# Weights split ahead of time into DRAM, and convolution taps summed in PSUM by TensorE and VectorE

## The chip, the cores and the metric

The program runs on one core of a Trainium2 chip. Its time is the device time of one execution in microseconds (us), and a version is judged by the median of several such executions. Engines are named as in the profile: PE (TensorE), DVE (VectorE), ACT (ScalarE), POOL (GpSimd), SP (SyncE, which here only issues transfers); PEld are PE's weight loads.

## The reference, cut to what matters

Two transformer blocks follow one another on 512 tokens of 1024 features, all in float32. The stage that the change is about is the pooling and convolution mixer of the second block; beside it, the keys and values of the memory for the second cross attention come from `m @ wkv`.

```python
def pool_conv_mixer(h, w_in, pool_w, pool_scale, dw_w, dw_b, ln_g, ln_b, w_out):
    z = h @ w_in                                        # 1024 -> 512 + 512 + 512
    u, glu_a, glu_b = jnp.split(z, [POOL_W, POOL_W + CONV_W_2], axis=-1)
    ug = u.reshape(b, t, N_POOL_GROUPS, POOL_GROUP)     # 4 groups, windows 2, 4, 8, 16
    pooled = jnp.stack([window_mean_minus_self(ug[:, :, i], w) ...], axis=2)
    ya = jnp.einsum("btgc,gcd->btgd", pooled, pool_w).reshape(b, t, POOL_W) * pool_scale
    gl = glu_a * jax.nn.sigmoid(glu_b)
    cv = causal_dwconv(gl, dw_w) + dw_b                 # 31 taps for each of 512 channels
    yb = jax.nn.silu(layernorm(cv, ln_g, ln_b))
    return jnp.concatenate([ya, yb], axis=-1) @ w_out
...
    k, v = jnp.split(m @ wkv, 2, axis=-1)               # m: 256 rows of normed memory
```

The stages in order are mix1, ffn1 (first block), pool, xa0, ffn2a, mla, xa1, ffn2b with the output (second block).

## The kernel before

Activations are feature-major: a tile holds 128 features by 512 tokens. A float32 product is made of three products in a reduced float32 (fp32r): each operand is split into a high part `hi` and a low part `lo`, and `mm3` (L239 to L242) sums hi·hi, lo·hi and hi·lo in PSUM. So each weight block is loaded by SP (`ws`, L228), then split: ACT writes `wh` (L211), DVE writes `wl` (L212); `ws`, `wh` and `wl` have three buffers each. A scheduler places the instructions of each engine; the splits are given a priority ahead of the products that need them (`AHEAD`, 150 steps in the pool stage).

**ffn1** (`ffn`, L1193) runs over 22 blocks of 128 hidden features. Each takes a gate and an up block (24 products each), a three-tap convolution, a gelu and a product; then eight output blocks of 66 products follow (`PostNorm`), three weight loads each. `PostNorm.apply` then takes the norm of the result: PE sums squares (L300), a power gives the factor per token, PE spreads it over the partitions (`bcast_cols`, L321), DVE and POOL scale (L477), DVE adds x (L479), and ACT and DVE split the next stage's operand into `nh` (L217) and `nl` (L218), tile by tile.

**The pool stage** (`pool_mix`, L1240) needs twelve column blocks of `w_in`, in the order of `ORDER`: `p` is a pooling group, `g` a pair of gate and value blocks of the convolution, `w` a product with `pool_w`. For a group g POOL makes the window sums (L1295), DVE subtracts (L1300), and `ph`/`pl` are split. For a convolution channel block, the gated tile `gl` (L1260) is summed over 31 taps: DVE takes 87 taps of the four blocks in SBUF (L1279), POOL takes 29 of its own (L1277), ACT the first and the last. When `cv` of all four is there, PE sums them over the channels (L1345, four matmuls against a matrix of ones), ACT and DVE make the layer norm with another sum of squares and another spreading, and the result is split again (`ypart`) for the output product `residual`. PSUM has eight banks: six for blocks (`mm`), two for sums (`aux`).

**Memory K/V of the second layer** (`mem_kv` with `plain=True`) are plain float32 products of 256 columns: eight blocks of K (L633), four of V (L645). They are PE's filling work: `PNF`, `PFILL` and `LNF` say after which step of `apply`, of the pool stage and of the layer norm a piece is emitted. Their weights go through `ws`; results are stored in DRAM (L619).

SP issues all of these loads and stores in one row; one that must wait (for a free buffer, or for data to be stored) holds back all behind it.

## Time and profile before

| | us |
|---|---|
| median of three runs | 2208.73 (2205.94 to 2208.89) |
| span of the profiled execution | 2204.3 |
| PE busy | 2107.7 (96%) |
| DVE busy | 1251.6 (57%) |
| ACT busy | 931.9 (42%) |
| POOL busy | 419.4 (19%) |

The profiled execution is one of its own; its span lies 1.6 us under the fastest and 4.4 us under the median of the timed runs. PE is busy nearly everywhere, so what counts are the stretches where it is not. The table of stretches gives, for each, the time in which PE had work; the timeline gives each gap with what ended it. The pool stage runs from 760.8 us (the last product of ffn1) to 991.8 us (the last product of its output).

### The profile page before, as it was taken

The page shows a single profiled execution, that of the slowest core. Times are in us where ns is not written, and L with a number is a line of the kernel's source. Part 1 is how long each engine was busy: PE and PEld are TensorE (multiplying, and loading weights), DVE is VectorE, ACT ScalarE, POOL GpSimd, SP SyncE. Part 2 cuts the span into 40 slices and gives each one's busy share as a digit, 9 for nine tenths or more (in the row PEclk, how much of TensorE's full clock was granted, in tenths as well). Part 3 has the DMA queues.
Part 4 walks back from the last instruction along what each step waited for, and adds up shares of the span by engine and source line. Part 5 has one row for each costly group of instructions (what it writes and reads, how often), then busy time and mean ns, then how long its engine had stood idle before and what let it go on. Part 6 is the DMA issues. An engine that isn't in the chain of part 4 may idle for free.

```text
span 2204.3 us, 27463 instructions
## 1 busy us (share of the span) xinstructions
PE 2107.7 (96%) x10615; PEld 1779.8 (81%) x10615; DVE 1251.6 (57%) x1796; ACT 931.9 (42%) x1527; POOL 419.4 (19%) x437
## 2 busy tenths in 40 slices
PE   8999999999999987799999999999999999999998
PEld 6988888788888865688888888888888888888887
DVE  6556864655542189955665554337885565555432
ACT  5675444433333253253443333225774343333322
POOL 2114422211100156420111110012322011111010
PEclk9999999999999998899999999999999999999999
DMA  5443235233333232372133333332124213333231
GB/s 162 144 154 104 77 109 178 87 96 96 96 98 112 83 115 62 101 229 86 53 91 96 97 100 98 114 106 56 27 82 157 86 49 92 99 96 96 89 104 66
DMA packets 369983, 222.86 MB, mean 101 GB/s; under 512 B 22407, under 2 KB 351036, under 8 KB 369852
## 3 DMA queue, kind: packets, MB, share of 16 engines
q1 hardware_dynamic: 366304, 219.65, 33.0%
q8 instruction: 83, 1.36, 0.3%
q10 hardware_dynamic: 3228, 1.42, 0.2%
q14 instruction: 48, 0.39, 0.1%
q0 software_dynamic: 320, 0.04, 0.0%
HBM read 201.41 MB, written 19.66 MB: 100 GB/s over the span
## 4 chain that ended last, share of the span: by engine, by line
PE 48%; DVE 4%; ACT 3%; issue 2%; POOL 1%; DMA 0%; SPq 0%; POOLq 0%; ACTq 0%; DVEq 0%
PE mm L242 13%; PE mm L240 13%; PE mm L241 13%; PE st L240 1%; PE st L241 1%; PE st L242 1%; PE nd L240 1%; PE nd L241 1%; PE nd L242 1%; ACT pr L1648 1%; DVE wl L212 1%; DVE c L1647 1%; PE aux L321 0%; DVE ptl L212 0%; DVE qt L212 0%
## 5 line engine op out<-in xcount | busy, mean ns | idle before, releaser
L211 ACT ACTIVATE wh<-ws 128x1024 fp32r<-128x1024 f32 (+2 forms) x336 | 344.8, 1028 | 747.9 <-PE mm L242 548.5
L212 DVE TENSOR_TENSOR wl<-ws,wh 128x1024 fp32r<-128x1024 f32 (+2 forms) x336 | 405.9, 1208 | 314.1 <-ACT wh L211 314.1
L240 PE MATMUL mm<-a,wh 128*128 128x512 f32 x1324 | 520.7, 393 | 0.8 <-ACT a L217 0.8
L242 PE MATMUL mm<-a,wh 128*128 128x512 f32 x1324 | 518.4, 392 | 1.1 <-DVE a L218 1.1
L241 PE MATMUL mm<-a,wl 128*128 128x512 f32 x1324 | 518.0, 391 | 0.3 <-DVE wl L212 0.2
L242 PEld LDWEIGHTS mm<-a,wh 128*128 128x128 f32 x1324 | 249.3, 188 | 54.1 <-DVE a L218 3.0
L240 PEld LDWEIGHTS mm<-a,wh 128*128 128x128 f32 x1324 | 249.7, 189 | 52.2 <-ACT a L217 1.7
L241 PEld LDWEIGHTS mm<-a,wl 128*128 128x128 f32 x1324 | 249.8, 189 | 51.6 <-DVE wl L212 1.0
L286 POOL TENSOR_TENSOR sq<-sq 128x512 f32<-128x512 f32 x62 | 98.8, 1594 | 632.0 <-ACT sq L281 530.9
L240 PE MATMUL mm<-hh,wh 128*128 128x512 f32 (+1 forms) x550 | 209.8, 381 | 0.0
L241 PE MATMUL mm<-hh,wl 128*128 128x512 f32 (+1 forms) x550 | 209.5, 381 | 0.0
L242 PE MATMUL mm<-hl,wh 128*128 128x512 f32 (+1 forms) x550 | 209.4, 381 | 0.0
L1223 POOL TENSOR_TENSOR t<-t,rb 128x512 f32<-128x512 f32 x66 | 85.3, 1293 | 626.5 <-ACT t L1222 626.5
L1210 DVE TENSOR_TENSOR t<-mm,rb 128x512 f32<-128x512 f32 x66 | 45.6, 691 | 152.3 <-PE mm L242 152.2
L1226 DVE TENSOR_TENSOR t<-mm,t 128x512 f32<-128x512 f32 x66 | 45.6, 692 | 143.4 <-POOL t L1223 143.4
L241 PEld LDWEIGHTS mm<-hh,wl 128*128 128x128 f32 x550 | 103.4, 188 | 19.7
L242 PEld LDWEIGHTS mm<-hl,wh 128*128 128x128 f32 x550 | 103.4, 188 | 19.7
L240 PEld LDWEIGHTS mm<-hh,wh 128*128 128x128 f32 x550 | 103.4, 188 | 19.7
L1219 DVE SCALAR_TENSOR_TENSOR t<-t,par 128x511 f32<-128x511 f32 (+1 forms) x132 | 98.7, 748 | 3.2 <-ACT t L1215 0.9
L1222 ACT ACTIVATE t<-t 128x512 f32<-128x512 f32 x66 | 41.7, 632 | 132.1 <-DVE t L1219 132.0
L1279 DVE SCALAR_TENSOR_TENSOR cv<-gl,par,cv 128x512 f32<-128x512 f32 x87 | 90.1, 1077 | 0.4
L240 PE MATMUL mm<-wh,a 128*128 128x256 f32 x282 | 82.2, 292 | 6.2 <-DVE f L838 3.9
(442 smaller groups left out, 3668.8 us busy)
## 6 DMA issues: line engine op xcount, KB each, us to landing
ws<-in_ffn_w_up_dram SPq DMA_DIRECT2D x110, 512.0 KB, 3.7
ws<-in_ffn_w_down_dram SPq DMA_DIRECT2D x48, 512.0 KB, 3.5
ws<-in_xa_wkv_dram SPq DMA_DIRECT2D x32, 512.0 KB, 4.1
ws<-in_w_in_dram SPq DMA_DIRECT2D x24, 512.0 KB, 5.0
ws<-in_ffn_w_gate_dram SPq DMA_DIRECT2D x22, 512.0 KB
ws<-in_ffn_w_down_dram SPq DMA_DIRECT2D x24, 384.0 KB, 3.0
ws<-in_xa_wq_dram SPq DMA_DIRECT2D x16, 512.0 KB, 5.6
ws<-in_xa_wo_dram SPq DMA_DIRECT2D x16, 512.0 KB, 3.5
```

The costliest lines, as they stand in the source:

```text
L211: SC.activation(out=hi, in_=src, func=ACTF.Copy)
L212: eng.tensor_tensor(out=lo, in0=src, in1=hi.bitcast(F32), op=ALU.subtract)
L240: PE.matmul(ps, lhsT=lh, rhs=rh, start=start, stop=False)
L241: PE.matmul(ps, lhsT=ll, rhs=rh, start=False, stop=False)
L242: PE.matmul(ps, lhsT=lh, rhs=rl, start=False, stop=stop)
L286: GP.tensor_tensor(out=self.acc, in0=self.acc, in1=self.new, op=ALU.add)
L1210: V.tensor_tensor(out=g, in0=pg, in1=rb, op=ALU.mult)
L1219: V.scalar_tensor_tensor(out=cv[:, o], in0=g[:, i], scalar=w, in1=cv[:, o], op0=ALU.mult, op1=ALU.add)
L1222: SC.activation(out=ge, in_=cv, func=func)
L1223: GP.tensor_tensor(out=ge, in0=ge, in1=rb, op=ALU.mult)
L1226: V.tensor_tensor(out=h, in0=pu, in1=ge, op=ALU.mult)
L1279: V.scalar_tensor_tensor(out=cv, in0=gl[:, j:j + S], scalar=w, in1=cv, op0=ALU.mult, op1=ALU.add)
```

## The change

- While ffn1 runs, 32 blocks are split ahead of time (`split_ahead`): the twelve of the pool stage's `w_in`, the four double tiles of the normed memory with the layer's gain, eight of K's weights and eight halves of V's. Each is loaded into `rs`, split (ACT into `rh`, DVE in place) and stored in DRAM as high and low part; there is one `rs` and one `rh`. One block is handled with each of the 22 gate/up blocks, the other ten with the output blocks.
- In the pool stage `get_halves` loads the two parts straight into `wh` and `wl` (for K's weights both into `ws` buffers): no split there. `pool_w` and `w_out` are still split there.
- Memory K/V are fp32r products by `mm3`: three of 256 columns for each float32 one before; the work is still PE's filling.
- `apply` calls `pool_open` after each tile: the first three `w_in` blocks (8, 4, 9) take the tile at once, in PSUM banks of their own (`op`). The final factor of the norm follows after the eighth tile.
- The convolution is summed in a PSUM bank (`cv`, two of them; `mm` has four in that stage): for the second to fourth channel block PE adds 5, 5 and 6 taps, each as one float32 product of a diagonal matrix (made by ACT) with the shifted `gl`; DVE adds its 24, 19, 19 and 18 taps with the PSUM bank as input and output; POOL has six taps of each block.
- The channel sums are made one by one, as each `cv` is there (`means`). The tables `ORDER`, `PNF`, `PFILL`, `TAPS` and `LNF` are new.

```diff
+PEC = (0, 5, 5, 6)
+ORDER = 'a1 b2 a2 b3 a3 p0 p2 p1 w0 p3 w2 w1 w3'
...
+    def split_ahead(pool, items):
+        for key, src, gains in items:
+            if callable(src):
+                src = src()
+            nk, n = src.shape[1], src.shape[2]
+            st = pool.tile([P, nk, n], F32, tag="rs", bufs=1, name="rs")
+            hi = pool.tile([P, nk, n], F32R, tag="rh", bufs=1, name="rh")
+            DMA.dma_start(out=st, in_=src)
+            lo = st.bitcast(F32R)
+            if gains is None:
+                split(hi, lo, st)
+            else:
+                for i, g in enumerate(gains):
+                    split(hi[:, i], lo[:, i], st[:, i], g)
+            yield
+            d = [dramp.tile([P, nk, n], F32, name=f"{key[0]}{z}" + "_".join(map(str, key[1:])))
+                 for z in "hl"]
+            DMA.dma_start(out=d[0], in_=hi.bitcast(F32))
+            DMA.dma_start(out=d[1], in_=st)
+            halves[key] = d
+            yield
+    def get_halves(key, kinds=("wh", "wl")):
+        ts = []
+        for d, kind in zip(halves[key], kinds):
+            t = w_tile(kind, d.shape, F32R)
+            DMA.dma_start(out=t.bitcast(F32), in_=d)
+            ts.append(t)
+        return ts
...
+                if each:
+                    each(nm, c)
+            if not each:
+                return nm.finish()
+            self.fill(2 * KD + 3)
+            r = nm.ss.rstd(D)
+            self.fill(2 * KD + 4)
+            nm.finish(r)
+            self.fill(2 * KD + 5)
+            return nm
...
+    def kv_ahead(l):
+        w = A["xa_wkv_2"][l]
+        for k in range(KD // 2):
+            yield (("mem", l, k), lambda k=k: mem_x[k], [pc("mem", KD * l + 2 * k + z) for z in range(2)])
+        for c in range(KD):
+            yield ("kw", l, c), w[:, c * P:(c + 1) * P].rearrange("(k p) c -> p k c", p=P), None
+        for c in range(4):
+            for k in (0, 4):
+                yield (("vw", l, c, k), w[k * P:(k + 4) * P, D + c * 2 * P:D + (c + 1) * 2 * P]
+                       .rearrange("(k p) c -> p k c", p=P), None)
...
+    def mem_kv_ahead(l, tag):
+        parts = []
+        for k in range(KD // 2):
+            hl = [act_tile((P, 2, 2 * P)) for _ in range(2)]
+            for t, d in zip(hl, halves["mem", l, k]):
+                DMA.dma_start(out=t.bitcast(F32), in_=d)
+            parts.extend((hl[0][:, z], hl[1][:, z]) for z in range(2))
+        yield
...
+            wh, wl = get_halves(("kw", l, c), ("ws", "ws"))
+            ps = pm(tag, (P, 2 * P))
+            for k in range(KD):
+                mm3(ps, wh[:, k, :], wl[:, k, :], *parts[k], k == 0, k == KD - 1)
...
+                wh, wl = get_halves(("vw", l, c, k0))
+                for t in range(2):
+                    ts = slice(t * P, (t + 1) * P)
+                    for k in range(4):
+                        ah, al = parts[k0 + k]
+                        mm3(ps[:, t], ah[:, ts], al[:, ts], wh[:, k, :], wl[:, k, :],
+                            k0 + k == 0 and t == 0, k0 + k == KD - 1 and t == 1)
...
             for f in range(KF):
                 pg = lin_f(wg, f * P, parts)
+                drain(pre, 1)
...
                 hs.append((hh, hl))
+                drain(pre, 1)
...
+            def both(i):
+                if i < KD:
+                    drain(pre, 2 if i < KD - 1 else None)
+                (fill or (lambda i: None))(i)
...
+        psum_phase(op=3, mm=3, aux=2)
+        return pn.apply(nxt, None, pp[0], pool_open)
...
+    def pool_ahead():
+        wi = A["pc_w_in_2"][0]
+        for c in (8, 4, 9, 5, 10, 6, 11, 7, 0, 2, 1, 3):
+            yield ("pw", c), wi[:, c * P:(c + 1) * P].rearrange("(k p) c -> p k c", p=P), None
+    def pool_products(blk, k, nm):
+        ps, (wh, wl) = blk
+        mm3(ps, wh[:, k, :], wl[:, k, :], *nm.parts[k], k == 0, k == KD - 1)
+    def pool_open(nm, k):
+        if k == 0:
+            opened.extend((pm("op"), get_halves(("pw", c))) for c in (8, 4, 9))
+        for blk in opened:
+            pool_products(blk, k, nm)
...
+        own = {c: {1 + i * 30 // POOLC[c] for i in range(POOLC[c])} for c in range(4)}
+        dia = {c: [j for j in range(1, 31) if j not in own[c]][:PEC[c]] for c in range(4)}
+        def conv_pe(c):
+            gl = gls[c]
+            cps[c] = pm("cv")
+            for n, j in enumerate(dia[c]):
+                dg = pp.tile([P, P], F32, tag="dgc", bufs=3, name="dgc")
+                SC.activation(out=dg, in_=ident, func=ACTF.Copy, scale=pc("dw_w", 4 * j + c))
+                PE.matmul(cps[c], lhsT=dg, rhs=gl[:, j:j + S], start=n == 0,
+                          stop=n == PEC[c] - 1)
+        def conv(c):
+            gl, ps = gls[c], cps[c]
+            c2 = pp.tile([P, S], F32, tag="c2", bufs=2, name="c2")
+            SC.activation(out=c2, in_=gl[:, 0:S], func=ACTF.Identity, scale=pc("dw_w", c),
+                          bias=pc("dw_b", c))
+            fresh = not PEC[c]
+            for j in range(1, 31):
+                w = pc("dw_w", 4 * j + c)
+                if j in own[c]:
+                    t = pp.tile([P, S], F32, tag="cm", bufs=4, name="cm")
+                    SC.activation(out=t, in_=gl[:, j:j + S], func=ACTF.Copy, scale=w)
+                    GP.tensor_tensor(out=c2, in0=c2, in1=t, op=ALU.add)
+                elif j in dia[c]:
+                    continue
+                elif fresh:
+                    V.tensor_scalar(out=ps, in0=gl[:, j:j + S], scalar1=w, scalar2=None,
+                                    op0=ALU.mult)
+                    fresh = False
+                else:
+                    V.scalar_tensor_tensor(out=ps, in0=gl[:, j:j + S], scalar=w, in1=ps,
+                                           op0=ALU.mult, op1=ALU.add)
+                yield
...
-            V.tensor_tensor(out=cv, in0=cv, in1=c2, op=ALU.add)
+            V.tensor_tensor(out=cv, in0=ps, in1=c2, op=ALU.add)
...
+        def means():
+            while len(sums) < len(cvs):
+                c = len(sums)
+                if c == 0:
+                    means.ps = pm("aux")
+                sums.append(c)
+                PE.matmul(means.ps, lhsT=ones, rhs=cvs[c], start=c == 0, stop=c == 3)
...
-            psum_phase(mm=6, aux=2)
+            psum_phase(mm=4, cv=2, aux=2)
```

How the instructions stand. First SP within ffn1, gate/up blocks. Before, with what each waits for (DMAHW: an earlier transfer landed; DVE, Activation: that engine is done with a tile):

```order
L227 DMA ws<-in_ffn_w_up_dram 128x8x128 [waits DMAHW2_49,DMAHW1_49,DVE_49]
L227 DMA ws<-in_ffn_w_gate_dram 128x8x128 [waits DMAHW3_49,DVE_49]
L227 DMA ws<-in_ffn_w_up_dram 128x8x128 [waits DMAHW6_49,DVE_49]
L227 DMA ws<-in_ffn_w_gate_dram 128x8x128 [waits DMAHW4_49,DMAHW1_49,DVE_49]
L227 DMA ws<-in_ffn_w_up_dram 128x8x128 [waits DMAHW5_49,DMAHW2_49,DVE_49]
L227 DMA ws<-in_ffn_w_gate_dram 128x8x128 [waits DMAHW3_49,DVE_49]
```

The same place now; `rs` and `rh` are the single buffers, `pwh`/`pwl` the parts in DRAM:

```order
L227 DMA ws<-in_ffn_w_up_dram 128x8x128 [waits DMAHW5_49,DVE_49]
L251 DMA rs<-in_pc_w_in_dram 128x8x128 [waits DMAHW6_49,DMAHW4_49]
L227 DMA ws<-in_ffn_w_gate_dram 128x8x128 [waits DMAHW0_49,DVE_49]
L261 DMA pwh_4481<-rh 128x1024 [waits Activation_49]
L262 DMA pwl_4482<-rs 128x1024 [waits DMAHW1_49,DVE_49]
L227 DMA ws<-in_ffn_w_up_dram 128x8x128 [waits DMAHW2_49,DVE_49]
L251 DMA rs<-in_pc_w_in_dram 128x8x128 [waits DMAHW3_49,DMAHW1_49]
L227 DMA ws<-in_ffn_w_gate_dram 128x8x128 [waits DMAHW5_49,DVE_49]
```

Between two weight loads there now stand a load of `rs` that waits for the two stores ahead of it to land, or two stores that wait for ACT's and DVE's split.

Next PE at the end of ffn1, the last product and what follows. Before (`a` are the memory's tiles, `sq` the squares, `dg` the diagonals of the token factors):

```order
L242 MATMUL mm_6393<-hl21_5746,wh_6456 128x512
L633 MATMUL mm_6489<-a_5927,ws_6487 128x256 x2
L633 MATMUL mm_6489<-a_5928,ws_6487 128x256 x2
L633 MATMUL mm_6489<-a_5929,ws_6487 128x256 x2
L633 MATMUL mm_6489<-a_5930,ws_6487 128x256 x2
L300 MATMUL aux_6503<-ones_79,sq_5836 128x1 x4
L300 MATMUL aux_6503<-ones_79,sq_6480 128x1 x4
L633 MATMUL mm_6537<-a_5927,ws_6535 128x256 x2
L633 MATMUL mm_6537<-a_5928,ws_6535 128x256 x2
L321 MATMUL aux_6520<-dg_6521,ones_79 128x128
L321 MATMUL aux_6520<-dg_6524,ones_79 128x128
```

Now (`a_6763` and `a_6764` are the high and low part of the memory's first tiles, `mm_6783` is the first block of K):

```order
L277 MATMUL mm_6646<-hl21_5948,wh_6709 128x512
L335 MATMUL aux_6851<-ones_79,sq_6042 128x1 x4
L335 MATMUL aux_6851<-ones_79,sq_6733 128x1 x4
L356 MATMUL aux_6902<-dg_6903,ones_79 128x128
L356 MATMUL aux_6902<-dg_6906,ones_79 128x128
L356 MATMUL aux_6902<-dg_6909,ones_79 128x128
L356 MATMUL aux_6902<-dg_6912,ones_79 128x128
L275 MATMUL mm_6783<-a_6763,ws_6779 128x256
L276 MATMUL mm_6783<-a_6763,ws_6781 128x256
```

Before, K products stood between the sum and the spreading of the norm; now they stand behind both. A little further on, PE's row now reads (`op` are the banks of `pool_open`):

```order
L276 MATMUL mm_6783<-a_6771,ws_6781 128x256
L277 MATMUL mm_6783<-a_6772,ws_6779 128x256
L276 MATMUL op_6998<-nh0_6989,wl_7001 128x512
L275 MATMUL mm_6783<-a_6775,ws_6779 128x256
L276 MATMUL mm_6783<-a_6775,ws_6781 128x256
L277 MATMUL op_6993<-nl0_6990,wh_6994 128x512
L277 MATMUL op_6998<-nl0_6990,wh_6999 128x512
L275 MATMUL op_6993<-nh1_7021,wh_6994 128x512
```

The first block of K is not finished before products that take `nl0`, the low part of the first operand tile, have been issued.

Last, PE at the layer norm's end. Before (`7650` and `7688` are blocks of the output product):

```order
L241 MATMUL mm_7650<-a_7329,wl_7654 128x512
L242 MATMUL mm_7650<-a_7330,wh_7653 128x512
L321 MATMUL aux_7611<-dg_7612,ones_79 128x128
L321 MATMUL aux_7611<-dg_7615,ones_79 128x128
L240 MATMUL mm_7650<-a_7366,wh_7653 128x512
L241 MATMUL mm_7650<-a_7366,wl_7654 128x512
L242 MATMUL mm_7650<-a_7367,wh_7653 128x512
L240 MATMUL mm_7688<-a_7310,wh_7691 128x512
L241 MATMUL mm_7688<-a_7310,wl_7692 128x512
L321 MATMUL aux_7611<-dg_7618,ones_79 128x128
L321 MATMUL aux_7611<-dg_7621,ones_79 128x128
L242 MATMUL mm_7688<-a_7311,wh_7691 128x512
```

Now (`8312` is the last output block that is opened before the layer norm's operands are there):

```order
L335 MATMUL aux_8180<-ones_79,sq_8167 128x1 x4
L335 MATMUL aux_8180<-ones_79,sq_8177 128x1 x4
L275 MATMUL mm_8312<-a_7768,wh_8315 128x512
L276 MATMUL mm_8312<-a_7768,wl_8316 128x512
L277 MATMUL mm_8312<-a_7769,wh_8315 128x512
L275 MATMUL mm_8312<-a_7800,wh_8315 128x512
L276 MATMUL mm_8312<-a_7800,wl_8316 128x512
L277 MATMUL mm_8312<-a_7801,wh_8315 128x512
L356 MATMUL aux_8197<-dg_8198,ones_79 128x128
L356 MATMUL aux_8197<-dg_8201,ones_79 128x128
L356 MATMUL aux_8197<-dg_8204,ones_79 128x128
L356 MATMUL aux_8197<-dg_8207,ones_79 128x128
```

Behind the spreading (L356) PE's next row is now a product of `a_8214`, the first operand that the layer norm gives; before, 27 products of the pooled half stood between the spreading's first rows and that operand.

## Rows read from the trace of the kernel before

**Rows 1.** the three stretches (PEclk: granted clock; DMA: busy share)

```profile
core 0: us, PE busy (x) PEld busy (x) DVE busy (x) ACT busy (x) POOL busy (x), PEclk, DMA share, GB/s
411.00:760.80 349.80, 349.80 (x1546) 289.71 (x1545) 150.29 (x175) 122.22 (x154) 36.62 (x32) 1.00 0.33 98
760.80:949.60 188.80, 151.95 (x641) 122.58 (x640) 159.46 (x192) 67.88 (x106) 95.54 (x72) 0.89 0.33 101
949.60:991.80 42.20, 42.20 (x192) 35.00 (x190) 24.03 (x30) 22.35 (x31) 10.24 (x6) 1.00 0.76 231
```

**Rows 2.** timeline of PE, waits in the pool stage (start, length, [idle before])

```profile
784.96 0.80 PE L241 MATMUL mm<-nh,wl 128*128 128x512 f32 x1 [5.78 <-DVE wl L212]
...
886.62 0.79 PE L240 MATMUL mm<-ph,wh 128*128 128x512 f32 x1 [6.25 <-ACT ph L211]
...
926.61 2.08 PE L1345 MATMUL aux<-cv,ones 128*128 128x512 f32 x2 [6.40 <-DVE cv L1282]
```

**Rows 3.** groups by line, 760.8 to 949.6 (count | busy us, mean ns)

```profile
L1279 DVE SCALAR_TENSOR_TENSOR cv<-gl,par,cv 128x512 f32<-128x512 f32 x87 | 90.1, 1077 | 0.4
...
L212 DVE TENSOR_TENSOR wl<-ws,wh 128x1024 fp32r<-128x1024 f32 (+1 forms) x15 | 20.9, 1396 | 2.0 <-ACT wh L211 2.0
...
L218 DVE SCALAR_TENSOR_TENSOR a<-mm,par,a 128x512 fp32r<-128x512 f32 x4 | 3.0, 742 | 1.5 <-ACT a L217 1.5
...
L1260 DVE TENSOR_TENSOR gl<-mm,t 128x512 f32<-128x512 f32 x4 | 2.7, 681 | 1.9 <-PE mm L242 1.9
```

**Rows 4.** timeline of DVE, taps of the convolution

```profile
920.58 5.38 DVE L1279 SCALAR_TENSOR_TENSOR cv<-gl,par,cv 128x512 f32<-128x512 f32 x8
```

**Rows 5.** timeline of PE, the forms of product

```profile
375.95 0.28 PE L242 MATMUL mm<-wl,mhl 128*128 128x256 f32 x1
376.07 0.28 PE L240 MATMUL mm<-wh,mhl 128*128 128x256 f32 x1
...
937.09 1.02 PE L1345 MATMUL aux<-cv,ones 128*128 128x512 f32 x2
937.94 7.07 PE L645 MATMUL mm<-ws,a 128*128 128x256 f32 x32
```

**Rows 6.** timeline of PE, the norm before the pool stage

```profile
764.25 1.84 PE L300 MATMUL aux<-ones,sq 128*128 128x1 f32 x16
...
768.45 0.68 PE L321 MATMUL aux<-dg,ones 128*128 128x128 f32 x4 [0.52 <-DVE dg L320]
```

**Rows 7.** timeline of DVE, the same norm

```profile
770.68 2.37 DVE L477 TENSOR_TENSOR a<-a,rb 128x512 f32<-128x512 f32 x2 [1.22 <-ACT rb L326]
...
773.30 6.46 DVE L479 TENSOR_TENSOR x<-a,x 128x512 f32<-128x512 f32 x4
```

**Rows 8.** timeline of DVE, one block of the first FFN

```profile
505.32 0.69 DVE L1210 TENSOR_TENSOR t<-mm,rb 128x512 f32<-128x512 f32 x1 [2.52 <-PE mm L242]
506.42 1.23 DVE L212 TENSOR_TENSOR wl<-ws,wh 128x1024 fp32r<-128x1024 f32 x1 [0.40 <-ACT wh L211]
...
516.20 0.69 DVE L1210 TENSOR_TENSOR t<-mm,rb 128x512 f32<-128x512 f32 x1 [2.52 <-PE mm L242]
```

**Rows 9.** timeline of ACT, the same block

```profile
505.32 1.06 ACT L211 ACTIVATE wh<-ws 128x1024 fp32r<-128x1024 f32 x1 [3.61 <-PE mm L242]
```

**Rows 10.** line 844, the stores of 512 KB before 300 us

```profile
DMA to landing us min/median/max: 2.7/3.3/4.4
```

**Rows 11.** line 227, the weight loads from 411 to 762 us

```profile
DMA to landing us min/median/max: 3.0/3.6/3.9
```

**Rows 12.** DMA issues from 940 to 990 us

```profile
ws<-in_xa_wq_dram SPq DMA_DIRECT2D x5, 512.0 KB, 7.7
```

**Rows 13.** timeline of PE, the tail of the layer norm

```profile
949.17 0.71 PE L321 MATMUL aux<-dg,ones 128*128 128x128 f32 x4 [0.30 <-DVE dg L320]
```

**Rows 14.** timeline of DVE, the same tail

```profile
955.33 0.69 DVE L212 TENSOR_TENSOR a<-cv,a 128x512 fp32r<-128x512 f32 x1 [0.26 <-ACT a L211]
```

**Rows 15.** the chain that ended last, end of the pool residual

```profile
991.88 0.79 PE aux L300 x8
```

More of the change, by code (lines that the diff above doesn't have):

```diff
@@ L1245, in pool_mix, with block, gate @@
                      .to_broadcast([P, 4, 16]))
-        cvs, us, yparts = {}, {}, {}
-        def glu(c):
-            pb = lin_f(wi, D + c * P, parts, eng=GP if c in UW else V)
+        gls, cps, cvs, us, yparts, sgs = {}, {}, {}, {}, {}, {}
+        def block(c):
+            blk = pm("mm"), get_halves(("pw", c))
+            for k in range(KD):
+                pool_products(blk, k, nm)
+            return blk[0]
+        def gate(c, pb):
             sg = ptmp()
@@ L1286, in pooled @@
         def pooled(g):
[L1287 removed]
+            ps = block(g)
             with tc.high_priority(offset=HPU[0]):
@@ L1322, in pool_w @@
                 ypart(ps, pc("pool_scale", g), g)
-            yield
-        taps = []
         def all_taps():
-            for i in range(4):
-                while len(taps) <= i:
+            for c in range(4):
+                while c not in cps:
                     yield
-                yield from taps[i]
-        conv_steps = all_taps()
-        gen = {"p": pooled, "g": glu, "w": pool_w}
-        mains = itertools.chain(*(gen[a](int(b)) for a, b in ORDER.split()))
-        for n, _ in enumerate(mains):
-            drain(conv_steps, TAPS[0] if taps else 0)
+                yield from conv(c)
+        sums = []
+        def means():
[5 more added lines that the diff above has]
+                PE.matmul(means.ps, lhsT=ones, rhs=cvs[c], start=c == 0, stop=c == 3)
+        (pb0, _), (pa0, _), (pb1, _) = opened
+        gate(0, pb0)
+        value(0, pa0)
+        gate(1, pb1)
+        taps = all_taps()
+        due = [0]
+        for n, a in enumerate(ORDER.split()):
+            kind, c = a[0], int(a[1])
+            ready = len(cvs)
+            if kind == "p":
+                pooled(c)
+            elif kind == "w":
+                pool_w(c)
+            elif kind == "b":
+                gate(c, block(D // P + c))
+            else:
+                value(c, block(S // P + c))
+            while due:
+                conv_pe(due.pop())
+            if kind == "a":
+                due.append(c)
+            drain(taps, TAPS[0])
+            if ready:
+                means()
             drain(fill, PFILL[n])
         while len(cvs) < 4:
-            drain(conv_steps, TAPS[1])
-            drain(fill, 1)
-        ps = pm("aux")
-        for c in range(4):
-            PE.matmul(ps, lhsT=ones, rhs=cvs[c], start=c == 0, stop=c == 3)
+            drain(taps, TAPS[1])
+            if len(cvs) < 4:
+                drain(fill, 1)
+        means()
         drain(fill, LNF[0])
         mean = ptmp()
-        SC.activation(out=mean, in_=ps, func=ACTF.Copy, scale=1.0 / S)
+        SC.activation(out=mean, in_=means.ps, func=ACTF.Copy, scale=1.0 / S)
         ss = SumSq()
@@ L1742 @@
     pcs, pp = ExitStack(), []
-    fills = itertools.chain(*(
-        mem_kv(l, range(12), "mm", plain=True) for l in where.get("pool", ())))
+    kv_late = where.get("pool", ())
+    fills = itertools.chain(*(mem_kv_ahead(l, "mm") for l in kv_late))
     def post_fill(i):
```

119 lines of the change are left out of this document (43 added, 76 removed).

## The prediction

> **What bounds the kernel now.** I first read the page: PE is busy for 96% of the span, so a change pays where PE stands still or runs slowly. The table of stretches says where [rows 1]: from 411 to 760.8 us, most of the first FFN, PE has no idle time at all (1546 products in 349.80 us, 0.2263 us each) while the transfers take 0.33 of the DMA engines; from 760.8 to 949.6 us PE works for 151.95 of 188.80 us, so it is idle for 36.85, and its clock was granted at 0.89; from there to 991.8, where the next sum of squares shows the end of the output product [rows 15], it is never idle. The timeline of PE names what ended the gaps [rows 2]: a split of weights on VectorE (5.78 us at 784.96), the split of a pooling group on ScalarE (6.25 at 886.62), the last tap of a convolution block (6.40 at 926.61). The groups by line give VectorE's load in that stretch [rows 3]: 87 taps take 90.1 us, 15 weight splits 20.9. So the pool stage is bound by PE waiting for VectorE's row and for chains through it; the first FFN is bound by PE alone.
>
> **The change part by part.** I sum PE's time from 760.8 to 991.8, which is 231.0 us.
>
> Before, PE's products in it are worked out at full rate. Memory K/V: 256 float32 products at 7.07 / 32 = 0.221 us [rows 5], 56.6. Twelve blocks: 288 × 0.2263 = 65.2. Items that stay: 12 products with pool_w 2.7, four channel sums at 937.94 − 937.09 = 0.85 each [rows 5] 3.4, three sums of squares at 1.84 and five half spreadings at 0.68 [rows 6] 8.9, nine output products before 949.6 2.0; together 17.0. The sum is 138.8; PE was busy for 151.95, so 13.1 went to products at the lower of the two clock levels, which follow the long gaps. 138.8 + 13.1 + 36.85 + 42.2 = 231.0.
>
> Now, work. Memory K/V: 384 fp32r products of 256 columns at 376.07 − 375.95 = 0.12 us [rows 5], 46.1, so 10.5 less. Diagonals: 16 float32 products of 512 columns, like a channel sum, at 0.85: 13.6 more (up to 1.04 each, 16.6, at 2.08 for two records in the slow stretch [rows 2]). The rest is as before: 46.1 + 65.2 + 13.6 + 17.0 + 42.2 = 184.1 us.
>
> Now, waits. The gaps of before go: the twelve w_in blocks are no longer split there, so that of the fifteen VectorE splits in the stretch [rows 3] only those of pool_w and w_out stay. Their place is taken by these.
> - Start of the stage. The memory's operands are loaded by SP behind a `wl` buffer that PE frees only with its last FFN product at 760.8, and K products stand behind the norm's spreading in PE's row. The first operand's low part is at the end of VectorE's chain: two scalings 2.37 and four additions 6.46 from 770.68 [rows 7], ending at about 779.7; the spreading is 1 to 2 us earlier without the K products inside it, so about 778. Until then PE has 17.3 us and, by its row, about 5.6 us of work (sum of squares, spreading, 21 K products, four block products). I take 11.7 idle; the bounds are 6 (the first operand comes 4 us sooner and K's tiles are there) and 15.
> - Second operand tile, and K's weights. Two reloads of 512 KB for each K block go through three `ws` buffers, each landing in 3.6 us [rows 11], against 24 × 0.12 = 2.9 us of products. I take 3.8 + 1.8; bounds 0 and 12 (another 1.4 for each of five blocks).
> - The second norm: nothing stands between its sum of squares and its spreading, 768.45 − 764.25 − 1.84 = 2.4 [rows 6]; taken 2.3, bounds 0 and 2.4.
> - The fourth pooling group: pool_w's product still waits for `ph`. Taken 5, bounds 0 and 6.25 [rows 2].
> - The layer norm's end. Before, 36 output products filled the time from the sum of squares on; now 30 of them stand ahead of it, in the place of V products. From the spreading at 949.17 to the first operand, 955.33 + 0.69 = 956.0 [rows 13, 14], is 6.9 us, of which the spreading takes 2.2 and 4.7 are empty; with 1.1 ahead of it and three waits of 0.45 behind, 7.2. Bounds 3 and 9.
>
> They add up to 31.8. At the lower clock I take 5 us lost, an estimate: in proportion to the idle time it would be 13.1 × 31.8 / 36.85 = 11.3, but the loss follows each long gap once, and the new idle time lies in three long ones (the first, the pooling group's, the layer norm's); bounds 3 and 11. 184.1 + 31.8 + 5.0 = 220.9, so 10.1 us less than 231.0.
>
> VectorE's taps. 80 instead of 87, with one input and the output in PSUM. No row shows VectorE writing PSUM. The bounds are 0.67, eight taps without POOL's company in 5.38 us [rows 4], and 1.08, the mean of all [rows 3]. I take 0.68, near the two rows with a PSUM input: 742 ns for one product-and-subtract standing alone and 681 for a product [rows 3]. Then the taps take 54 us instead of 90 and the convolution ends about when PE is through with its blocks; they add nothing to the sum.
>
> [...]
>
> The first FFN. 32 blocks add 1.06 us to ScalarE and 1.23 to VectorE each [rows 8, 9], and 1.5 MB: two stores and a load of 512 KB. Each gate/up block lasts 516.20 − 505.32 = 10.88 us [rows 8] and the two engines are busy for 122.22 and 150.29 of 349.80 us [rows 1], so this lies beside PE. Transfers rise from 98 GB/s by 1.5 MB in 10.88 us to some 235, about what 949.6 to 991.8 carries without PE waiting (231 GB/s, 0.76 of the engines [rows 1]). I take 0; if the cover fails, it is the first rival.
>
> So the profiled span would be 2204.3 − 10.1 = 2194.2, and as the median stands 4.4 us over it, 2198.6. I predict 2198.
>
> **The rivals.**
>
> *SP's row becomes the first FFN's bound.* With one `rs` and one `rh`, a load waits for both stores of the block before to land, and the weight loads for the FFN itself wait behind it in SP's row. One round is a load 3.6 [rows 11], ScalarE 1.06, VectorE 1.23, a store 3.3 [rows 10] and some 0.5 to 1 for handovers: 9.7 to 10.2 us. The period is 10.88 in the 22 gate/up blocks and, for the ten later ones that stand two weight loads apart, 66 × 0.2263 × 2 / 3 = 9.96. It fits by little. Bounds: 3.0 + 1.06 + 1.23 + 2.7 = 8.0 and, with 7.7 for a load in a crowded stretch [rows 12] and 4.4 for a store, 14.4. The buffers ahead hide about 11 us in all (an estimate, one block's period). A round of 12 would cost 22 × 1.12 + 10 × 2.04 − 11 = 34 us: 2232, slower than before; it decides from 11.3 on. For it speaks that the transfers more than double; against it that a load and a store seldom run at the same time and that 231 GB/s were carried. Chance 0.14.
>
> [...]
>
> *Taps in PSUM cost as much beside POOL as taps in SBUF.* At 1.08 us, VectorE's row is 80 × 0.41 = 33 us longer; POOL has 24 taps instead of 29, so 27; nearly all shows, as PE waited for VectorE at the end of the convolution before (6.40 [rows 2]): about 2223. It decides from 0.81 us a tap. Against it: instructions with a PSUM input stand at 681 and 742 ns in the same stretch [rows 3]. Chance 0.06.
>
> *The middle waits vanish.* If the reloads come early enough and the pooling group and the layer norm's end are covered by products that I count as late, only the first wait stays, with its share of lost clock: 20.1 less, 2178. For it: nothing is split in the stage any more, and DMA has 0.67 of its time free there [rows 1]. Against it: the waits at the norms rest on PE's row alone, which has nothing to fill them. Chance 0.20.
>
> **How the numbers follow.** My forecast has 0.60, with its own range from 2190 (waits 25, low bounds for half of them) to 2206 (waits 40). About 0.2%, 4.4 us, is what a measurement of this kernel can tell from no change: so faster means under 2204.3, slower over 2213.1. Faster: 0.52 of the forecast and 0.19 of the third rival, 0.71. Slower: 0.01 + 0.12 + 0.06 = 0.19 from the forecast's tail and the first two rivals. The remaining 0.10 is no change. The range that leaves 0.2 out goes from 2176, the third rival with a little more, to 2222, half-way into the first rival and up to the second.
>
> **What would show it.** In the new trace PE should have no idle time between 411 and 760.8; a gap there that a weight split or a load ended is the first rival. Taps should stand at 0.67 to 0.75 us whether POOL works or not; a mean over 0.9 is the second. In the pool stage the idle time of PE should be near 32 us, 10 to 12 of it within 18 us after the FFN's last product, about 7 at the layer norm's end, and no gap there ended by a split of w_in. K/V products should stand at 0.12 us. If idle time is under 15 us, the third rival holds; if PE's gaps at the start exceed 15 us, my reading of SP's row there was too kind.

## The result and the profile after

The changed kernel takes 2242.0 us (median of four runs, 2241.05 to 2245.99) against 2208.8: a ratio of 1.0155, 95% interval 1.0140 to 1.0171. It is slower, by 1.6%. Its profiled span is 2240.3 us, 36.0 more than before. The last product of the first FFN ends at 792.4 us instead of 760.8, so 31.6 us are lost up to there; the pool stage, from that product to the first sum of squares of its output, takes 236.2 us instead of 231.1; the rest of the program is 0.7 shorter.

The table of stretches of the changed kernel (columns as in [rows 1]) for the gate/up blocks of the first FFN and for the pool stage:

```profile
416.27:680.95 264.68, 248.64 (x1056) 200.11 (x1054) 144.24 (x178) 109.08 (x135) 30.71 (x22) 0.98 0.67 204
792.40:1028.60 236.20, 207.37 (x989) 169.68 (x988) 139.06 (x201) 78.81 (x132) 82.94 (x73) 0.90 0.54 184
```

In the FFN PE now has 16 us without work in 264.68 us, where it had none before [rows 1]. Of its busy 248.64 us some 9.6 are lost too: 1056 products at 0.2263 us would be 239.0, and products behind its gaps run at a lower clock: behind those of 1.32 and 1.75 us that end at 504.90 and 507.16, the granted clock was 0.50 from 508.6 to 511.2 us, with products 0.43 us apart; over the whole stretch it was 0.98. In the pool stage it has 28.8 without work and its clock was granted at 0.90.

The view of the line that takes in each gate block, before and now (count: shortest/median/longest ns, first and last start):

```profile
L1210 DVE TENSOR_TENSOR t<-mm,rb x22: 682/692/692, 412.1 to 635.9; 128x512 f32<-128x512 f32 x22
...
L1279 DVE TENSOR_TENSOR t<-mm,rb x22: 678/683/693, 416.3 to 669.8; 128x512 f32<-128x512 f32 x22
```

From the first to the last of 22 blocks are 253.5 us, 12.07 each; before, they were 223.8 us, 10.66 each. That is 29.7 of the 31.6 us. The first block comes 4.2 us later than before, and the eight output blocks take no longer: from the last start to the FFN's last product it is 122.6 us, against 124.9. Of the 4.2 us, 2.6 are there ahead of the FFN, where nothing was changed: this profile reaches the norm in front of it at 386.7 us, the one before at 384.1, and all others, e10 to e12 with the code of before too, at 385.9 to 388.6. PE's own gaps in the FFN are short; what waits is ScalarE (line waited for: us in total, times, longest):

```profile
ACT rh L211 <- DMA rs<-in_xa_wkv_dram: 88.5, 16, 7.9
ACT rh L211 <- DMA rs<-in_pc_w_in_dram: 36.9, 9, 5.6
```

ScalarE stood for 125 us in front of the split into `rh`, waiting for `rs` to land (a transfer lands when the last of its data is in place). Its timeline in two blocks:

```profile
487.24 1.06 ACT L211 ACTIVATE rh<-rs 128x1024 fp32r<-128x1024 f32 x1 [4.08 <-DMA rs<-in_pc_w_in_dram]
488.20 0.61 ACT L1291 ACTIVATE t<-t 128x512 f32<-128x512 f32 x1
...
500.18 1.06 ACT L211 ACTIVATE rh<-rs 128x1024 fp32r<-128x1024 f32 x1 [5.57 <-DMA rs<-in_pc_w_in_dram]
503.27 0.63 ACT L1291 ACTIVATE t<-t 128x512 f32<-128x512 f32 x1 [2.04 <-DVE t L1288]
```

L1291 is the FFN's gelu. It stands behind `rh` in ScalarE's row, so it waits with it: at 488.20 it starts right after that split, and at 503.27 it waits for a VectorE product that stands behind VectorE's part of the split. SP's row in the same stretch:

```profile
481.13 0.38 SPq L227 DMA_DIRECT2D ws<-in_ffn_w_up_dram  x1
481.61 0.53 SPq L251 DMA_DIRECT2D rs<-in_pc_w_in_dram  x1
...
488.32 0.34 SPq L261 DMA_DIRECT2D pwh<-rh  x1
489.58 0.34 SPq L262 DMA_DIRECT2D pwl<-rs  x1
492.58 0.38 SPq L227 DMA_DIRECT2D ws<-in_ffn_w_up_dram  x1
493.06 0.54 SPq L251 DMA_DIRECT2D rs<-in_pc_w_in_dram  x1
```

The load of `rs` at 481.61 is followed by its split only at 487.24. The stores go at 488.32 and 489.58, and the next load of `rs` follows at 493.06, right behind a weight load that VectorE's split had to release. The chain that ended last (start, length):

```profile
481.61 5.56 DMA rs<-in_pc_w_in_dram
...
488.89 1.82 POOL t L1292
...
491.34 1.23 DVE wl L212
...
493.06 7.01 DMA rs<-in_pc_w_in_dram
```

It goes from the landing of `rs` over ScalarE's split and gelu, POOL's product and VectorE's weight split to the weight load on SP and the next load of `rs`: a closed round, 11.45 us here and 14.55 the next time. From 455.90 to 559.06 eight such rounds took 12.9 us each on average, and a block of the FFN took as long. The landing is about half of a round. Of all loads of `rs`, those whose landing the view can tell:

```profile
DMA to landing us min/median/max: 2.7/5.0/5.4
```

On the chain the loads of 512 KB in the steady rounds took 5.1 to 7.0 us.

The store is not in this round. SP's waits from 411 to 690 us, the time of the gate/up blocks, and then the landings of the stores of low parts up to 560 us, where the view can tell them:

```profile
SPq L227 <- DVE wl L212: 102.3, 41, 4.2
...
SPq L251 <- DMA pwl<-rs: 2.3, 1, 2.3
```

```profile
DMA to landing us min/median/max: 2.7/2.7/2.7
```

The store at 489.58 landed 0.8 us before the next load of `rs` was issued, the one at 502.53 2.4 us before. Of the 19 loads of weight blocks into `rs` in that time one waited for a store, by 2.3 us; the others went as soon as SP had issued the weight load ahead of them, and that waited for VectorE's weight split. In the output blocks, from 690 us on, it is the other way about:

```profile
SPq L251 <- DMA vwl<-rs: 10.0, 7, 1.7
```

There each load waits for the store ahead of it, and a round takes 9.2 to 11.1 us.

Now the pool stage. PE's timeline at its start:

```profile
801.86 0.28 PE L277 MATMUL mm<-a,ws 128*128 128x256 f32 x1
801.98 0.28 PE L275 MATMUL mm<-a,ws 128*128 128x256 f32 x1
...
805.69 0.80 PE L275 MATMUL op<-nh,wh 128*128 128x512 f32 x1 [3.31 <-ACT nh L217]
806.28 0.63 PE L276 MATMUL op<-nh,wl 128*128 128x512 f32 x1
806.71 0.63 PE L275 MATMUL op<-nh,wh 128*128 128x512 f32 x1
```

Ahead of the gap that ends at 805.69, K products are 0.12 us apart. Behind it two products of 512 columns start 0.43 us apart, 1.9 times the 0.226 of [rows 1]: the granted clock was 0.50 from 805.69 to 808.40 us, against 1.00 from 816 to 830. So a gap costs more here than its length. Over the first 19.6 us of the stage the granted clock was 0.74. PE's waits in the whole stage (summed, times, longest):

```profile
PE aux L356 <- DVE dg L355: 4.9, 3, 2.4
PE mm L275 <- ACT a L211: 3.9, 1, 3.9
PE cv L1373 <- ACT dgc L1372: 3.8, 3, 2.0
PE mm L275 <- ACT ph L211: 3.6, 1, 3.6
PE op L275 <- ACT nh L217: 3.3, 1, 3.3
PE op L277 <- DVE nl L218: 2.2, 1, 2.2
```

No weight split is left among them, and VectorE's last tap isn't either. The taps (count | busy us, mean ns), and the shortest, median and longest of VectorE's before and now:

```profile
L1395 DVE SCALAR_TENSOR_TENSOR cv<-gl,par,cv 128x512 f32<-128x512 f32 x79 | 55.6, 750 | 0.9 <-PE cv L1373 0.2
...
L1387 POOL TENSOR_TENSOR c<-c,cm 128x512 f32<-128x512 f32 x24 | 32.1, 1339 | 2.5 <-ACT cm L1386 1.0
```

```profile
L1279 DVE SCALAR_TENSOR_TENSOR cv<-gl,par,cv x87: 735/746/1783, 815.4 to 934.6; 128x512 f32<-128x512 f32 x87
...
L1395 DVE SCALAR_TENSOR_TENSOR cv<-gl,par,cv x79: 742/750/756, 865.7 to 954.8; 128x512 f32<-128x512 f32 x79
```

79 taps take 55.6 us, 0.704 each, where 87 took 90.1, 1.04 each [rows 3]. The median hardly changed; what is gone is the long ones. POOL's own taps, before:

```profile
L1277 POOL TENSOR_TENSOR c<-c,cm 128x512 f32<-128x512 f32 x29 | 47.8, 1647 | 19.8 <-ACT c L1269 13.1 <-ACT cm L1276 4.9
```

They fell from 1647 to 1339 ns.

### The profile page after: what moved, and what is told of

It is laid out like the page before. It is cut to its first block, busy times and chain, and to the rows that moved or that the text cites. A ratio compares the mean times of both kernels' runs of the same rounds, so it can differ in the third digit from the quotient of the medians.

```text
span 2240.3 us, 28076 instructions
## 1 busy us (share of the span) xinstructions
PE 2131.4 (95%) x10775; PEld 1794.1 (80%) x10775; DVE 1238.5 (55%) x1813; ACT 946.7 (42%) x1551; POOL 400.6 (18%) x432
## 4 chain that ended last, share of the span: by engine, by line
PE 60%; DVE 11%; DMA 9%; issue 8%; ACT 7%; POOL 5%; SPq 0%; ACTq 0%; POOLq 0%; DVEq 0%
PE mm L277 16%; PE mm L275 16%; PE mm L276 15%; DMA rs<-in_xa_wkv_dram 3%; DMA rs<-in_pc_w_in_dram 2%; DVE wl L212 2%; PE st L275 1%; PE st L276 1%; PE st L277 1%; PE nd L275 1%; PE nd L276 1%; PE nd L277 1%; POOL t L1292 1%; POOL c L1387 1%; ACT rh L211 1%
## 5 line engine op out<-in xcount | busy, mean ns | idle before, releaser
L211 ACT ACTIVATE wh<-ws 128x1024 fp32r<-128x1024 f32 (+2 forms) x324 | 330.6, 1024 | 598.4 <-PE mm L277 390.8
L212 DVE TENSOR_TENSOR wl<-ws,wh 128x1024 fp32r<-128x1024 f32 (+2 forms) x324 | 387.0, 1197 | 235.1 <-ACT wh L211 235.0
L275 PE MATMUL mm<-wh,a 128*128 128x256 f32 x346 | 101.5, 294 | 7.1 <-DVE f L905 3.9
L212 DVE TENSOR_TENSOR rs<-rs,rh 128x1024 fp32r<-128x1024 f32 x28 | 34.3, 1225 | 127.0 <-ACT rh L211 127.0
L277 PE MATMUL mm<-wl,a 128*128 128x256 f32 x346 | 101.5, 293 | 1.2 <-DMA wl<-vwl 1.2
L276 PE MATMUL mm<-wh,a 128*128 128x256 f32 x346 | 100.8, 291 | 0.0
```

Of the source, the lines that this page charges most:

```text
L211: SC.activation(out=hi, in_=src, func=ACTF.Copy)
L212: eng.tensor_tensor(out=lo, in0=src, in1=hi.bitcast(F32), op=ALU.subtract)
L275: PE.matmul(ps, lhsT=lh, rhs=rh, start=start, stop=False)
L276: PE.matmul(ps, lhsT=ll, rhs=rh, start=False, stop=False)
L277: PE.matmul(ps, lhsT=lh, rhs=rl, start=False, stop=stop)
```

## The experiments

The first question was the FFN's 31.6 us, the second the pool stage. All ratios are to the kernel before, timed again beside each run (medians 2208.2 to 2209.7 us), with 95% intervals; runs are compared with each other by these ratios. Several kernels leave work out and serve for timing only; the text says what they leave out.

**e1, three items.** All blocks of one kind read the parts of the first one.

```diff
+            if key[0] in first:
+                halves[key] = halves[first[key[0]]]
+                yield
+                yield
+                continue
```

> Only one block of each of three kinds is split in the first FFN and all the others read its parts (the output is then not the reference's); the pool stage keeps its instructions. Both theories of the FFN's loss (the loop through the one rs buffer; the added transfers) expect the FFN's last product near 760 to 765 us instead of 792. The theory that the pool stage itself is some 5 us longer (29 us idle and about 20 us lost at the lower clock after some nine waits) expects it to keep its 236 us and the whole about 2211 us, equal to or just above the kernel before. Rival: the pool stage is slow only because of what the FFN leaves behind; then it falls under 225 us and the whole under 2200.

2214.9 us, ratio 1.0020 (1.0011 to 1.0029). PE's first sums of squares of the two norms around the pool stage:

```profile
765.35 0.95 PE L342 MATMUL aux<-ones,sq 128*128 128x1 f32 x8
...
1000.23 0.95 PE L342 MATMUL aux<-ones,sq 128*128 128x1 f32 x8
```

The FFN is back (765.4; the 4.6 us over the profile before are there ahead of it), and the pool stage still takes 234.9 us. So the pool stage by itself is no faster than before.

**e2, no split.** Loads and stores as they are, nothing for ScalarE and VectorE.

```diff
-            if gains is None:
-                split(hi, lo, st)
-            ...
...
-            DMA.dma_start(out=d[0], in_=hi.bitcast(F32))
+            DMA.dma_start(out=d[0], in_=st)
```

> The loads and both stores of the 32 blocks stay, ScalarE's and VectorE's split of them is left out (so the stored parts are wrong). Loop theory (a block of the FFN lasts 12.3 us because load, split, stores and the FFN's own gelu follow one another through single buffers and in-order rows): with the split gone the block returns to about 10.9 us, the FFN ends near 765, the whole near 2213. Transfer theory (the traffic of about 210 GB/s itself starves the FFN's weights): the block stays over 12 us and the whole near 2240.

2214.5 us, ratio 1.0020 (1.0007 to 1.0033). The stretch of [rows 1]:

```profile
411.00:760.80 349.80, 349.80 (x1545) 289.49 (x1544) 150.97 (x177) 119.80 (x147) 36.43 (x32) 1.00 0.75 229
```

229 GB/s, and PE has no idle time: the transfers alone cost the FFN nothing. That theory falls. Without the split the stores wait for the load alone, so the round is shorter here too.

**e3, one store.**

```diff
-            DMA.dma_start(out=d[1], in_=st)
-            halves[key] = d
+            halves[key] = [d[0], d[0]]
```

> The split stays, the low part is not stored (the high part is read in its place, so the result is wrong). If the loop runs through the stores that must land before rs is loaded again, a round falls to some 5 + 1.1 + 1.2 us and the block returns to 10.9: about 2213. If it runs through ScalarE's row, where the split stands ahead of the FFN's gelu and the next weight split and load stand behind that (landing + 6.1 us), the block stays near 11 to 12 us: 2215 to 2238. Transfer theory, four fifths of the added traffic left: about 2235.

2219.8 us, ratio 1.0050 (1.0035 to 1.0066). ScalarE's waits for `rs`:

```profile
ACT rh L211 <- DMA rs<-in_xa_wkv_dram: 22.1, 16, 3.8
ACT rh L211 <- DMA rs<-in_pc_w_in_dram: 12.8, 10, 3.9
```

35 us in place of 125, and a block takes 10.85 us. Without the second store `rs` is free as soon as VectorE is done, and its load moves ahead of the weight load in SP's row; the run cuts both links of the round, the store's landing and SP's row. Which of them held it in the changed kernel is told by that kernel's own trace (above): SP's row.

**e4, pieces.** 64 pieces of half the size, three `rs`, one `rh`, a load one piece ahead.

```diff
-            st = pool.tile([P, nk, n], F32, tag="rs", bufs=1, name="rs")
...
+                p.append(pool.tile(list(p[3]), F32, tag="rs", bufs=3, name="rs"))
+                DMA.dma_start(out=p[4], in_=p[0])
```

> Every block is handled in two pieces of 256 KB with three rs buffers of half the size (same space) and one rh; a piece is loaded before the piece ahead of it is split. Loop theory: a load no longer waits for the stores just ahead, ScalarE waits under 1 us a piece, the FFN ends at 761 to 768 and the whole is 2211 to 2218. Transfer theory: the same bytes move, so 2235 or more.

2241.3 us, ratio 1.0139 (1.0122 to 1.0156): a miss. ScalarE's waits:

```profile
ACT rh L211 <- DMA pwh<-rh: 31.7, 15, 4.6
```

They moved to the one `rh`: the split now waits for the store of the piece before. The loads of `rs`:

```profile
DMA to landing us min/median/max: 2.6/3.1/4.2
```

**e5, two and two.** The same with two `rs` and two `rh`.

```diff
-... tag="rs", bufs=3 ... tag="rh", bufs=1
+... tag="rs", bufs=2 ... tag="rh", bufs=2
```

The edit is shown against e4.

> Pieces of 256 KB as in the run before, but two rs and two rh buffers of half the size in place of three and one. Loop theory, now naming the store's landing ahead of the next use of the buffer as the link that fails: one piece's round is load 3.5 + ScalarE 0.63 + VectorE 0.69 + store 2.7 + about 1 = 8.5 us, so two buffers give a piece each 4.3 us where the FFN needs one in 5.44; ScalarE's waits for stores go and the whole is 2212 to 2218, as with three items. Row theory (any split whose load or store lands late holds up ScalarE's row, whatever the buffers): 2230 or more.

2251.2 us, ratio 1.0189 (1.0167 to 1.0211): slower still, and my numbers for a round were wrong. The chain in a block:

```profile
481.30 3.59 DMA pwl<-rs
...
484.91 4.12 DMA rs<-in_pc_w_in_dram
```

and the landings of its loads of `rs`:

```profile
DMA to landing us min/median/max: 2.1/4.4/5.1
```

Here the store's landing is a link: the load of `rs` follows the store from the same buffer as soon as that has landed. A load of half the size lands in 4.4 us against 5.0 in the changed kernel, and the number of landings has doubled. In e4, with as many bytes a second from 411 to 790 us (213 GB/s, 210 here), the same loads landed in 3.1 us; so size alone does not set a landing, and what else does stays open.

**e9, three buffers.** `rs` and `rh` three times at full size, a load one block ahead; the space comes from hidden blocks 16 to 21 writing over the first six.

```diff
+                else:
+                    hh, hl = hs[f - 16]
...
+            (key, gains, st), nxt = nxt, load(next(it, None))
```

> Three rs and three rh buffers of full size, and each block's load issued one block ahead of its split. The space comes from the last six hidden blocks writing into the tiles of the first six, so the result is wrong; all products, splits, loads and stores stay. Theory as it stands after the half-size runs (a block's round of load, split and stores takes 12 to 13 us, and a round over the number of full buffers is what the FFN's 10.88 us is up against): 12.5 / 3 = 4.2 us, ScalarE's waits for rs fall from 125 us to under 15, the FFN ends near 762 to 768 and the whole is 2211 to 2219, as with three items. Row theory in its strong form (the extra splits and transfers in these rows cost the FFN its time even where nothing lands late): 2230 or more.

2219.7 us, ratio 1.0043 (1.0027 to 1.0059). ScalarE's waits for `rs`:

```profile
ACT rh L211 <- DMA rs<-in_xa_wkv_dram: 25.8, 14, 5.6
ACT rh L211 <- DMA rs<-in_pc_w_in_dram: 6.4, 4, 2.3
```

All splits, loads and stores are there, and a block takes 10.89 us. The landings of `rs`:

```profile
DMA to landing us min/median/max: 6.0/6.8/7.7
```

ScalarE's waits are above the 15 us I expected, but the FFN's last product ends at 767.4 us, 6.6 later than before instead of 31.6 (2.4 of them ahead of the FFN). The loads land later here than in the changed kernel (6.8 us against 5.0), so it is not a shorter landing that gave the FFN its pace back, but the number of rounds under way.

The runs on the FFN side by side; the block is the distance of the first from the last of 22, over 21, and ScalarE's waits are all that stand in front of a split into `rh` from 411 to 790 us, whatever ended them:

| | block, us | ScalarE's waits, us | whole, us |
|---|---|---|---|
| before | 10.66 | 0 | 2208.8 |
| after | 12.07 | 136 | 2242.0 |
| e1 three items | 10.60 | 4 | 2214.9 |
| e2 no split | 10.66 | 0 | 2214.5 |
| e3 one store | 10.85 | 41 | 2219.8 |
| e4 pieces | 11.79 | 113 | 2241.3 |
| e5 two and two | 12.07 | 125 | 2251.2 |
| e9 three buffers | 10.89 | 40 | 2219.7 |

The block follows ScalarE's waits, not the bytes.

**e6, no diagonals** (with three items).

```diff
-PEC = (0, 5, 5, 6)
+PEC = (0, 0, 0, 0)
```

> Three items split ahead (as in the first run, output wrong for that reason) and no diagonal products on PE: VectorE adds 96 taps instead of 80. If PE is what bounds the pool stage, the 32 records of the diagonals (16.2 us busy) go and the whole is 2199 to 2206; VectorE's 16 taps more at 0.70 are 11 us in a row that is busy for 139 of 236 us. If the convolution's end (VectorE) bounds, nothing is gained or it is slower: 2213 to 2222.

2214.3 us, ratio 1.0028 (1.0018 to 1.0038), as with the diagonals (2214.9, 1.0020). Two of PE's waits in the stage are new or longer:

```profile
PE aux L1462 <- DVE cv L1406: 6.0, 1, 6.0
PE aux L342 <- POOL sq L328: 5.7, 1, 5.7
```

The 32 records of the diagonals, 0.43 us each, are gone from PE. Its busy time in the stage fell by 11.4 us (205.7 to 194.3) and its waits rose by 14 (29.1 to 43.1), for VectorE's last tap and for POOL's sum behind it above all. **e8**, two and two buffers without diagonals, was to join both parts:

> Two and two buffers and no diagonals, everything computed. If both earlier theories hold (FFN's loss is the buffers' loop; PE bounds the pool stage), 2199 to 2207, faster than the kernel before. If only the pool part holds, 2226 to 2232; if neither, 2240.

2250.7 us, ratio 1.0186 (1.0167 to 1.0205), which is e5 again: neither part held, and both expectations had been written before e5 and e6 were known.

**e7, K early** (with three items).

```diff
-PNF = (0, 0, 0, 0, 0, 0, 0, 2, ...
+PNF = (0, 0, 0, 0, 0, 1, 0, 1, ...
```

> Three items split ahead (output wrong for that reason), and the loads of the memory's operands and the first K block are emitted during the FFN's last output blocks instead of after them. Theory that the pool stage's loss is its waits and the lower clock after each: of the first 20 us, 8.4 idle and about 4 lost at the lower clock, half to two thirds go: 2204 to 2209. Rival (the norm's own chain over VectorE ends at the same time, so the K block only moves the wait to the second norm, where 2.4 us are idle already): 2211 to 2216.

2209.7 us, ratio 1.0009 (1.0000 to 1.0018). That is 5 us under e1 by the medians, 2.4 by the ratios. The profiled pair shows 1.2 in the pool stage (233.7 against 234.9) and 1.8 ahead of it, where only loads were moved; waits at the start became shorter and others longer. I count it as inconclusive.

**e10, the taps alone.** The kernel before, with only the convolution moved to PSUM (four banks `mm`, two `cv`).

```diff
-            cv = pp.tile([P, S], F32, name=f"cv{c}")
+            cv = pm("cv")
...
-            V.tensor_tensor(out=cv, in0=cv, in1=c2, op=ALU.add)
-            cvs[c] = cv
+            done = pp.tile([P, S], F32, name=f"cv{c}")
+            V.tensor_tensor(out=done, in0=cv, in1=c2, op=ALU.add)
+            cvs[c] = done
...
-            psum_phase(mm=6, aux=2)
+            psum_phase(mm=4, cv=2, aux=2)
```

> The kernel before with one part of the change: the convolution of each channel block is summed in a PSUM bank by VectorE (two banks cv, four mm); everything else, the splits in the pool stage, POOL's 29 taps and the float32 K/V products, as before. Taps at 0.70 us in place of 1.08 take 29 us out of VectorE's row in the pool stage. If PE's gaps that VectorE's row ended (5.57, 5.93, 2.41, 6.40 us) were made by the slow taps, half to all of them go with part of the lower clock behind them: 2190 to 2203. Rival: with four banks for blocks in place of six the products wait for free banks instead: 2205 to 2216.

2192.5 us, ratio 0.9933 (0.9915 to 0.9951): faster than both. Between the medians are 17 us, by the ratio it is 15. Its taps, and PE's longest wait in the stage:

```profile
L1279 DVE SCALAR_TENSOR_TENSOR cv<-gl,par,cv 128x512 f32<-128x512 f32 x87 | 60.9, 746 | 0.3
```

```profile
PE mm L241 <- DVE wl L212: 6.9, 2, 5.8
```

87 taps take 60.9 us instead of 90.1. The waits for `wl` are 6.9 in all, 13.8 before; the one for the last tap, 6.40 [rows 2], is gone. The pool stage takes 215.5 us (760.9 to 976.4) against 231.1.

**e11, one bank** for the convolution, five for blocks.

> The same with one bank for the convolution and five for blocks. If the banks for blocks matter, faster than the run before by 2 to 6 us; if the next convolution block's start in a bank of its own matters, slower by 2 to 4.

2207.2 us, ratio 0.9993 (0.9984 to 1.0002). PE's longest wait:

```profile
PE mm L240 <- ACT wh L211: 10.9, 4, 7.7
```

The longest ends at 794.6 us, before the first tap (820.6): ScalarE waits there 4.4 us for a `w_in` block to land. In e10 it waits 4.2 us for the same block, but PE has products in its row meanwhile. The order of the stage's start changed with the banks, so the run doesn't tell what a bank of the convolution is worth.

**e12, POOL's taps** from 29 to 20 on top of e10 (`POOLC = (4, 6, 4, 6)`).

> The kernel with the convolution summed in two PSUM banks (2192.5 us), and POOL's own taps reduced from 29 to 20, so that VectorE has 96. In that kernel the longest waits of PE inside the pool stage are for a pooling group's split (4.98 us) behind POOL's window sums and for a VectorE result (4.77). If POOL's row is late because of its taps, 9 x 1.41 = 13 us come out of it and the whole is 2186 to 2192; if VectorE's row (9 taps more at 0.70, 6 us) sets the end, 2193 to 2200.

2202.0 us, ratio 0.9967 (0.9955 to 0.9979), by the ratios 7.5 us slower than e10. A new wait:

```profile
PE aux L1346 <- DVE cv L1283: 6.5, 1, 6.5
```

VectorE's last tap is late again. With POOL's share it is not, so POOL's taps are worth keeping where VectorE's are fast.

## Why the prediction was wrong

**The step that failed: "I take 0; if the cover fails, it is the first rival."** The cover in the first FFN was counted by the engines' free time and by a round of 9.7 to 10.2 us. In the gate/up blocks the steady rounds took 11.5 to 14.6. Two things in the sum were wrong. The load was 3.6, taken from a stretch of 98 GB/s; it was 5.0 in the median and 5.1 to 7.0 on the chain, where the load of `rs` lies between two weight loads. And the round has other links than I gave it. I had a store's landing of 3.3 close it; the stores landed in mostly 2.7, and in all but one of 19 rounds before SP was ready for the next load. What stands between a split and the next load is the gelu, POOL's product, VectorE's product and weight split, and a weight load on SP, because the split stands in ScalarE's row ahead of the gelu and the load of `rs` in SP's row behind that weight load. So the first rival, which I gave 0.14, came in its place, SP's row, but not by its condition, that a load waits for the stores of the block before to land. That held in the output blocks, and there the rounds of 9.2 to 11.1 us were near the sum and cost the FFN nothing.

That the rival's price of 34 us for a round of 12 is near the 31.6 lost is luck: it has 24.6 for the gate/up blocks and 20.4 for the output blocks, less 11 hidden; measured are 29.7 and nothing.

What is shown is that a split which waits for a late landing in a row that the FFN needs costs the FFN its pace, and that it ends when there are three full buffers and a load goes a block ahead (e9) or when the round is cut (e3).

`rs` landed 1.4 us later than the loads of [rows 11], 5.0 us against 3.6 in the median, with 204 GB/s moved against 98. In e2, at 229 GB/s, the same loads landed in 3.9 us (median), and in e9, at 227, in 6.8, so the bytes moved a second alone don't explain it here.

**"At the lower clock I take 5 us lost."** Mis-sized: 207.4 us busy less 184.1 of work at full rate are 23.3. I let only the three longest gaps pay. In the trace the products behind shorter ones, such as the 2.36 us that end at 797.22 and the 2.40 that end at 855.94, ran at a granted clock of 0.50 too (from 797.22 to 801.5 us and from 856.4 to 859.6), and over the first 19.6 us, where short pieces of work lie between gaps, the granted clock was 0.74. With this term alone right, the stage would have been forecast at 239.2 us, slower than the 231.0 before; e1 shows 234.9.

**The waits** were 28.8 us against 31.8 taken, in other portions: the start 8.3 (11.7), the second norm 2.5 (2.3), the reloads of K 2.4 (5.6), the pooling group 3.6 (5), the tail 1.8 and 3.9 (7.2), and two that I had not listed, 3.8 for ScalarE's diagonal matrices and 2.1 for the reloads of V's weights.

**The diagonals** were costed as 13.6 us of PE's work, and 32 records at 0.43 us are 13.7. e6 shows that they were worth nothing either way: without them PE waits for VectorE's last tap instead.

**The taps** came out right: 0.68 taken, 0.704 measured, and the second rival is dead. Its price was a little high, as 1.08 is the mean length of a record and 0.67 the distance between two starts; like for like the taps in SBUF took 1.04 each. The trace shows the gain on both engines: VectorE's taps longer than 756 ns are gone (the longest was 1783), and POOL's taps are down by 308 ns in the mean, from 1647 to 1339. What I missed is that this one part, alone on the kernel before, was worth 15 us (e10). In the changed kernel it was joined to parts that cost more than it gave; which of those in the pool stage cost most, the runs don't separate.

**The third rival** (the middle waits vanish) did not come: K's reload, the pooling group and the tail all still show.

## What to carry to other kernels

Work moved into a stage where every engine has time still needs its round (load, work, store, the next load) to fit between the places it takes in rows that the stage needs; write down link by link what the next load stands behind in those rows, sum the round with landings under the new traffic, and divide by the number of full buffers. Smaller pieces in the same space did not help here (e4, e5): twice as many landings had to be waited for. Try the parts of a large change one at a time: here the one that took 15 us off was hidden by the others.

## What the runs showed of the hardware

The time from issue to landing is not given by the size of a transfer: beside the FFN's weights, loads of 256 KB landed in 3.1 us (e4) and 4.4 us (e5), loads of 512 KB in 3.9 us (e2), 5.0 us (the changed kernel) and 6.8 us (e9), all medians. VectorE adds a product into PSUM, with PSUM as one input, in 0.70 us beside POOL, and its records lie between 742 and 756 ns (the changed kernel; 737 to 756 in e10); with two inputs in SBUF it took 1.04 us, the records lay between 735 and 1783 ns, and POOL's own additions beside it took 308 ns longer in the mean, 1647 against 1339 (the kernel before; 1414 in e10). Behind PE's gaps of 2.36 us (to 797.22), 3.31 us (to 805.69) and 2.40 us (to 855.94) the products ran at a granted clock of 0.50 (from 797.22 to 801.5 us, 805.69 to 808.4 and 856.4 to 859.6), against 1.00 from 816 to 830, with products of 512 columns 0.43 us apart in place of 0.226 and products of 256 columns 0.21 in place of 0.12.
